# Log-sum-exp over rows: the first load's two transfers cut at one row instead of half a row, the second of them in packets of three rows

## The chip, the cores and the metric

The kernel runs on one core of one Trainium2 chip. The metric is the device time of one execution in microseconds (us), the median of several runs. One core has the engines PE (TensorE), DVE (VectorE), ACT (ScalarE), POOL (GpSimd) and SP (SyncE, which here issues all the transfers), and 16 DMA engines that carry the transfers.

## The reference: what is computed

For each of the 32 x 512 = 16,384 rows of 1,024 float32 numbers, the logarithm of the sum of the exponentials:

```python
max_x = np.max(x, axis=-1, keepdims=True)
return (max_x.squeeze(-1) + np.log(np.sum(np.exp(x - max_x), axis=-1))).astype(np.float32)
```

The input is 67.1 MB, the output 64 KB.

## The kernel before

The maximum isn't taken: the kernel sums the exponentials directly, looks at the end whether a sum or a number is out of bounds, and has a second, slow way (line 328 on) for that case, which doesn't run on these inputs.

The 16,384 rows are laid over 128 partitions, 128 rows each; what the program calls a row of a partition is one of these 1,024 numbers (`d`), 4 KB. The first 112 rows of each partition lie one behind the other in HBM (`x_rows`, line 80), and likewise the last 16 (`x_rest`), so a piece of several rows of one partition is one contiguous stretch in HBM and one in SBUF.

`LOADS` (line 25) is the order of the work, written out by hand: 18 loads, each with its size in rows and what is done with them. The first four have 16 rows (8 MB each), and then they shrink to under half a row. A load goes into a ring of 48 rows a partition (`ring`). ACT takes the exponential of the landed rows in place (line 235), and one of three ways adds them up: R, DVE sums whole rows (line 246); F, POOL first adds the halves of each row (line 240) and DVE sums what is left (line 177); T, DVE adds halves and sums row by row (line 256). The last row is summed by ACT (line 209). Logarithms (lines 275, 288, 290) and two stores end the program.

`load` (line 136) issues each load on SP. Where it overwrites ring space, SP first waits for whoever last read that space (line 139), in practice DVE's sums. Each load has a semaphore of its own, `landed[i]`, to which each transfer adds 16; ACT waits until it has 16 times the number of the load's transfers (line 203), so ACT starts on the first load when both of its parts have landed. Only the first load has two parts (line 141), cut at `FIRST` elements of each partition:

```python
        parts = [(0, FIRST), (FIRST, size)] if i == 0 else [(0, size)]
```

With `FIRST = 512` the first part has 128 x 512 elements (256 KB) and the second 128 x 15,872 (7,936 KB). The transfers of the first three loads (`AHEAD = 3`, four transfers) need no wait; `start_early` (line 387) moves them to the head of SP's program, ahead of the barrier at which the engines start together. They stand there in the order first part, second part, second load, third load.

Of the kernel before, what the change touches and what calls it, by code (L numbers as in the profile page):

```python
# [16 lines left out]
B = 16  # L17
LATE = 119
AHEAD = 3
FIRST = 512  # L20

# [31 lines left out]
def kernel(  # L55
# [30 lines left out]
    def source(e0, size):  # L86
        assert e0 >= W * d or e0 + size <= W * d
        return x_rest[:, e0 - W * d : e0 - W * d + size] if e0 >= W * d else x_rows[:, e0 : e0 + size]
# [8 lines left out]
    def sbuf(name, cols, dtype=fp32, rows=P):  # L97
        return nc.alloc_sbuf_tensor(name, [rows, cols], dtype).ap()

    ring = sbuf("ring", RING * d)  # L100
# [35 lines left out]
    def load(i, here, done_before, size):  # L136
        for a, b, who, at in users:
            if a < here + size and b > here:
                sp.wait(who, at)
        users[:] = [u for u in users if not (u[0] < here + size and u[1] > here)]  # L140
        parts = [(0, FIRST), (FIRST, size)] if i == 0 else [(0, size)]
        return [
            nc.sync.dma_start(  # L143
                out=ring[:, here + a : here + b], in_=source(done_before + a, b - a)
            ).then_inc(landed[i], 16)
            for a, b in parts
        ]
# [38 lines left out]
    here = 0  # L186
    early_sum = 0
    done_before = 0
# [3 lines left out]
    for i, (size, ops) in enumerate(loads):  # L192
# [3 lines left out]
        if any(q < here + size and q + t * d > here for _, t, q, _ in folded):  # L196
            reduce_folded()
        dma = load(i, here, done_before, size)
        if i < AHEAD:
            first_loads.extend(x.ins for x in dma)  # L200
# [3 lines left out]
        for k, (how, s) in enumerate(ops):  # L204
            rows = ring[:, p : p + s * d].rearrange("p (c d) -> p c d", d=d)
            if how in "YZ":
# [3 lines left out]
                    out=last_exp[:, here - p : end - p], in_=ring[:, here:end], func=AF.Exp,  # L210
# [4 lines left out]
                here = end  # L215
# [5 lines left out]
            elif how == "A":  # L221
# [3 lines left out]
                    out=v, in_=v, func=AF.Exp, accum_out=sumexp[:, c : c + 1]  # L225
# [5 lines left out]
            else:  # L231
# [4 lines left out]
                here = upto  # L236
            if how == "F":
# [3 lines left out]
                    out=rows[:, :, 0:H], in0=rows[:, :, 0:H], in1=rows[:, :, H:d], op=ALU.add  # L241
                ))
                folded.append((c, s, p, at))
            elif how == "R":
                dve.wait(act, at)
                who = (dve, dve.did(nc.vector.reduce_sum(  # L246
                    out=sumexp[:, c : c + s], in_=rows, axis=AX.X
                )))
                users.append((p, p + s * d, *who))
            elif how == "T":  # L250
# [3 lines left out]
                for r in range(s):  # L254
                    lo = rows[:, r, 0:H]
                    who = (dve, dve.did(nc.vector.scalar_tensor_tensor(  # L256
                        out=lo, in0=lo, scalar=1.0, in1=rows[:, r, H:d],
# [13 lines left out]
            if c == LATE:  # L271
# [4 lines left out]
                    out=res[:, 0:W], in_=sumexp[:, 0:W], func=AF.Ln  # L276
# [14 lines left out]
        out=res[:, LAST:NC], in_=last_sum, func=AF.Ln, bias=sumexp[:, LAST:NC]  # L291
# [8 lines left out]
        out=clamped[:, LATE:NC], in0=sumexp[:, LATE:NC], scalar=LOW,  # L300
# [10 lines left out]
        out=over[:, 0:half], in0=last_piece[:, 0:half], scalar=CEILING,  # L311
# [16 lines left out]
    with nc.If(all_fine < 1):  # L328
# [5 lines left out]
        for c0 in range(0, NC, RING):  # L334
# [6 lines left out]
            for c1, c2 in ((c0, edge), (edge, c0 + s)):  # L341
                if c1 == c2:
                    continue
                nc.scalar.dma_start(
                    out=ring[:, (c1 - c0) * d : (c2 - c0) * d],
                    in_=source(c1 * d, (c2 - c1) * d),
# [4 lines left out]
                out=neg, in_=v, op=ALU.max, axis=AX.X, negate=True  # L351
# [3 lines left out]
                out=v, in0=v, in1=neg[:, :, None].to_broadcast([P, s, d])  # L355
# [5 lines left out]
                out=sumexp[:, c0 : c0 + s], in_=v, axis=AX.X  # L361
# [71 lines left out]
```

## Time and profile before

| | |
|---|---|
| median of 3 runs | 161.47 us (161.45 to 161.5) |
| the profiled execution | 161.67 us |
| its span in the trace | 160.3 us |
| DVE busy, ACT busy | 114.2 us, 114.5 us |
| POOL busy, PE busy | 37.3 us, 2.2 us |
| share of 16 DMA engines' span in the loads' and stores' queue | 97.7% |
| packets in that queue | 3024, with 67.18 MB |
| ACT starts on the load of 7 rows (4,096 elements and so on) | 130.87 us |
| engines let go by the barrier (DVE's first instruction, ACT's table load) | 2.9 us |

Times within the trace count from the start of the span. A row of a timeline has the start, the length, the engine, the line, the operation with its tiles, how many instructions were merged into the row, and in brackets how long the engine had stood still and for whom. `SPq` is SP's own sequence of instructions: its rows give the time in which SP issued a transfer, not the transfer. DMA packets are counted in the window in which they start, with their whole time, so a short window can show more than 100% of the engines or more GB/s than they move.

### The profile page before, as it was taken

What the parts mean: (1) busy time and instruction counts of PE and PEld (TensorE: products, weight loads), DVE (VectorE), ACT (ScalarE), POOL (GpSimd) and SP (SyncE); (2) the same over time, 40 slices, a digit from 0 to 9 for tenths busy, and PEclk for the clock granted to TensorE, in tenths of its full rate; (3) what the DMA queues carried; (4) which work ended last, traced back from release to release, by engine and by line L of the source; (5) the groups of instructions that cost most, each with busy time, mean ns of one, the idle gap of its engine ahead of it and who ended that gap; (6) DMA issues with size and microseconds to landing.
All of it is one profiled execution on the core that took longest, in us unless ns stands there. A gap on an engine that the chain in (4) does not pass through costs nothing.

```text
span 160.3 us, 221 instructions
## 1 busy us (share of the span) xinstructions
PE 2.2 (1%) x26; PEld 1.1 (1%) x26; DVE 114.2 (71%) x59; ACT 114.5 (71%) x31; POOL 37.3 (23%) x11
## 2 busy tenths in 40 slices
PE   0000000000000000000000000000000000000022
PEld 0000000000000000000000000000000000000011
DVE  0000000009999499994999859959999999999996
ACT  2000059990799708995099949991999989799996
POOL 0000000000000000000000994690004969891000
DMA  8996996996996996996999999999998999999992
GB/s 319 507 491 269 507 523 262 523 523 262 523 507 278 523 507 278 523 507 278 482 441 441 441 425 409 409 409 489 432 432 371 451 416 435 416 413 425 415 410 87
DMA packets 3025, 67.18 MB, mean 419 GB/s; under 512 B 592, under 2 KB 720, under 8 KB 1488
## 3 DMA queue, kind: packets, MB, share of 16 engines
q1 hardware_dynamic: 3024, 67.18, 97.7%
q14 instruction: 1, 0.01, 0.0%
HBM read 67.11 MB, written 0.07 MB: 419 GB/s over the span
## 4 chain that ended last, share of the span: by engine, by line
DMA 52%; ACT 28%; DVE 19%; issue 1%; SPq 1%; PE 0%
DMA ring<-in_x_dram 52%; ACT ring L235 27%; DVE sumexp L246 15%; DVE sumexp L177 2%; DVE ring L256 1%; SPq L143 1%; DVE over L310 0%; PE count L315 0%; ACT res L275 0%; DVE clamped L299 0%; DVE fine L317 0%; DVE sumexp L219 0%
## 5 line engine op out<-in xcount | busy, mean ns | idle before, releaser
L235 ACT ACTIVATE ring<-ring 128x16384 f32<-128x16384 f32 (+16 forms) x23 | 111.7, 4908 | 41.5 <-DMA ring<-in_x_dram 41.5
L246 DVE TENSOR_REDUCE sumexp<-ring 128x16 f32<-128x16384 f32 (+4 forms) x9 | 85.6, 9513 | 41.2 <-ACT ring L235 41.2
L240 POOL TENSOR_TENSOR ring<-ring 128x3072 f32<-128x3072 f32 (+3 forms) x7 | 37.1, 5314 | 107.3 <-ACT ring L235 107.3
L177 DVE TENSOR_REDUCE sumexp<-ring 128x6 f32<-128x3072 f32 (+3 forms) x7 | 18.4, 2657 | 0.0
L256 DVE SCALAR_TENSOR_TENSOR ring<-ring 128x512 f32<-128x512 f32 x15 | 9.6, 687 | 0.4 <-ACT ring L235 0.4
L127 ACT ACT_TABLE_LOAD x1 | 1.3, 1283 | 2.9 <-PEq L64 2.9
L162 PE MATMUL count<-far,bad 128*1 128x1 f32 x2 | 0.2, 164 | 153.1 <-DVE clamped L157 153.1
L128 DVE MEMSET ones<- 128x1 f32 x1 | 0.1, 59 | 2.9 <-PEq L64 2.9
L166 PE MATMUL count<-sumexp,ones 128*1 128x1 f32 x18 | 1.6, 164 | 3.6 <-DVE ring L256 3.6
L256 DVE DVE_READ_ACCUMULATOR ring<-ring 128x1 f32 x15 | 1.2, 81 | 0.0
L209 ACT ACTIVATE last_exp<-ring 128x544 f32<-128x544 f32 (+1 forms) x2 | 1.2, 584 | 0.0
L162 PEld LDWEIGHTS count<-far,bad 128*1 128x1 f32 x2 | 0.1, 80 | 153.1 <-DVE clamped L157 153.1
L166 PEld LDWEIGHTS count<-sumexp,ones 128*1 128x1 f32 x18 | 0.8, 80 | 4.4 <-DVE ring L256 4.4
L310 DVE SCALAR_TENSOR_TENSOR over<-ring 128x240 f32<-128x240 f32 x1 | 0.4, 404 | 0.0
L317 DVE TENSOR_SCALAR fine<-count 1x1 int32<-1x1 f32 x1 | 0.1, 145 | 0.3 <-PE count L315 0.3
L157 DVE SCALAR_TENSOR_TENSOR clamped<-clamped,sumexp 128x119 f32<-128x119 f32 x1 | 0.3, 281 | 0.0
L275 ACT ACTIVATE res<-sumexp 128x112 f32<-128x112 f32 x1 | 0.3, 279 | 0.0
L290 ACT ACTIVATE res<-last_sum,sumexp 128x1 f32<-128x1 f32 x1 | 0.3, 262 | 0.0
L209 ACT ACTIVATION_READ_ACCUMULATOR last_exp<-ring 128x1 f32 x2 | 0.2, 124 | 0.0
L152 DVE TENSOR_SCALAR clamped<-sumexp 128x119 f32<-128x119 f32 x1 | 0.2, 221 | 0.0
L288 ACT ACTIVATE res<-sumexp 128x15 f32<-128x15 f32 x1 | 0.2, 207 | 0.0
L299 DVE SCALAR_TENSOR_TENSOR clamped<-sumexp 128x9 f32<-128x9 f32 x1 | 0.2, 169 | 0.0
(17 smaller groups left out, 1.8 us busy)
## 6 DMA issues: line engine op xcount, KB each, us to landing
ring<-in_x_dram SPq DMA_DIRECT2D x1, 7936.0 KB, 21.5
ring<-in_x_dram SPq DMA_DIRECT2D x1, 6912.0 KB, 23.9
ring<-in_x_dram SPq DMA_DIRECT2D x1, 6400.0 KB, 19.7
ring<-in_x_dram SPq DMA_DIRECT2D x1, 4608.0 KB, 15.9
ring<-in_x_dram SPq DMA_DIRECT2D x1, 3584.0 KB, 24.0
ring<-in_x_dram SPq DMA_DIRECT2D x1, 3072.0 KB, 19.1
ring<-in_x_dram SPq DMA_DIRECT2D x1, 2288.0 KB, 24.1
ring<-in_x_dram SPq DMA_DIRECT2D x1, 1664.0 KB, 20.9
```

Source lines behind the costliest of these rows:

```text
L127: nc.scalar.preload_act_table_set("natural_log_exp_and_others")
L143: nc.sync.dma_start(out=ring[:, here + a : here + b], in_=source(done_before + a, b - a)).then_inc(landed[i], 16)
L157: dve.did(nc.vector.scalar_tensor_tensor(out=clamped[:, 0:LATE], in0=clamped[:, 0:LATE], scalar=0.0, in1=sumexp[:, 0:LATE], op0=ALU.bypass ...
L162: pe.did(nc.tensor.matmul(count, lhsT=bad[:, 0:1], rhs=far, start=True, stop=False))
L166: return pe.did(nc.tensor.matmul(count, lhsT=ones, rhs=sumexp[:, c : c + 1], **kw))
L177: at = dve.did(nc.vector.reduce_sum(out=sumexp[:, c0 : c0 + s0], in_=halves, axis=AX.X))
L209: at = act.did(nc.scalar.activation(out=last_exp[:, here - p : end - p], in_=ring[:, here:end], func=AF.Exp, accum_out=first_sum if how == ...
L235: at = act.did(nc.scalar.activation(out=v, in_=v, func=AF.Exp))
L240: at = pool.did(nc.gpsimd.tensor_tensor(out=rows[:, :, 0:H], in0=rows[:, :, 0:H], in1=rows[:, :, H:d], op=ALU.add))
L246: who = (dve, dve.did(nc.vector.reduce_sum(out=sumexp[:, c : c + s], in_=rows, axis=AX.X)))
L256: who = (dve, dve.did(nc.vector.scalar_tensor_tensor(out=lo, in0=lo, scalar=1.0, in1=rows[:, r, H:d], op0=ALU.mult, op1=ALU.add, accum_out ...
L310: dve.did(nc.vector.scalar_tensor_tensor(out=over[:, 0:half], in0=last_piece[:, 0:half], scalar=CEILING, in1=last_piece[:, half : 2 * half ...
```

## The change

The first part has one row of each partition (4 KB) instead of half a row, and the second 15 rows instead of 15.5. The second part is given a limit of 12,288 bytes for the last dimension of its transfer. The other loads, the waits and the computation are as they were; the new constant and the new argument shift the later lines by one or two.

```diff
-FIRST = 512
+FIRST = 1024
+STEP = 12288
...
         parts = [(0, FIRST), (FIRST, size)] if i == 0 else [(0, size)]
         return [
             nc.sync.dma_start(
-                out=ring[:, here + a : here + b], in_=source(done_before + a, b - a)
+                out=ring[:, here + a : here + b], in_=source(done_before + a, b - a),
+                **({"max_dma_last_dim": STEP} if a else {}),
             ).then_inc(landed[i], 16)
             for a, b in parts
         ]
```

On SP the head of the program is, before (partitions x elements; `ring` is the ring, `in_x_dram` the input; the branch ends the part ahead of the barrier, and the load behind it is the fourth):

```order
L143 DMA ring<-in_x_dram 128x512
L143 DMA ring<-in_x_dram 128x15872
L143 DMA ring<-in_x_dram 128x16384 x2
L428 UNCONDITIONAL_BRANCH
L143 DMA ring<-in_x_dram 128x16384
```

and now:

```order
L144 DMA ring<-in_x_dram 128x1024
L144 DMA ring<-in_x_dram 128x5x3072
L144 DMA ring<-in_x_dram 128x16384 x2
L430 UNCONDITIONAL_BRANCH
L144 DMA ring<-in_x_dram 128x16384
```

The second instruction has five pieces of 3,072 elements (12,288 bytes) for each partition where it had one of 15,872 elements (63,488 bytes). No instruction changed its place, on SP or on another engine.

## Prediction

> **What bounds the kernel now.** I read the page's head and its chain of waits first, then the sums of waits, then ACT's and SP's rows in order of time, and last the DMA packets in short windows.
>
> ```profile
> span 160.3 us, 221 instructions
> DMA 52%; ACT 28%; DVE 19%; issue 1%; SPq 1%; PE 0%
> ACT ring L235 <- DMA ring<-in_x_dram: 41.5, 8, 17.8
> ```
>
> Half of the chain that ends last is transfers into the ring, and ACT, the first engine to touch the data, stood still 41.5 us in 8 waits, all for landings. The longest wait, 17.8 us, is for the load that the change edits. ACT's rows (start, length) show the beat of these landings:
>
> ```profile
> 21.92 13.86 ACT L235 ACTIVATE ring<-ring 128x16384 f32<-128x16384 f32 x1 [17.77 <-DMA ring<-in_x_dram]
> 41.27 13.86 ACT L235 ACTIVATE ring<-ring 128x16384 f32<-128x16384 f32 x1 [5.50 <-DMA ring<-in_x_dram]
> 60.62 13.86 ACT L235 ACTIVATE ring<-ring 128x16384 f32<-128x16384 f32 x1 [5.50 <-DMA ring<-in_x_dram]
> 79.97 13.95 ACT L235 ACTIVATE ring<-ring 128x9216 f32<-128x9216 f32 x2 [5.49 <-DMA ring<-in_x_dram]
> ```
>
> The second, third and fourth loads of 16 rows each come 19.35 us behind the one ahead. The first comes at 21.92, so the start of the program costs 21.92 - 19.35 = 2.57 us over the beat. The change can touch only that excess and the beat of its own load. Next question: does a shift at 21.92 reach the end whole? The chain in order of time (start, length), beginning and end:
>
> ```profile
> 0.00 0.39 SPq L143
> 0.39 0.05 issue
> 0.44 0.42 SPq L143
> 0.86 0.04 issue
> 0.90 40.35 DMA ring<-in_x_dram
> ...
> 72.41 23.88 DMA ring<-in_x_dram
> 96.28 0.02 issue
> ...
> 119.06 19.09 DMA ring<-in_x_dram
> 138.16 0.02 issue
> 138.18 12.34 ACT ring L235 x5
> 150.52 0.18 ACT res L275
> 150.70 6.04 ACT ring L235 x4
> ```
>
> The last landing that ACT waits for ends at 138.16. From there ACT computes without a pause and the tail follows. For a shift to go missing, the transfers would have to stand idle somewhere for want of an issue. SP's issues of the fourth load, of the sixth (12.5 rows), and of the pair whose first lands at 138.16:
>
> ```profile
> 53.06 0.33 SPq L143 DMA_DIRECT2D ring<-in_x_dram  x1
> ...
> 91.76 0.33 SPq L143 DMA_DIRECT2D ring<-in_x_dram  x1
> ...
> 119.06 0.80 SPq L143 DMA_DIRECT2D ring<-in_x_dram  x2
> ```
>
> The fourth load is issued at 53.06, 7.6 us before the third has landed (60.62). The sixth is issued at 91.76, 4.5 us before the fifth lands (the chain's 96.28), and the pair at 119.06 comes 11.8 us before ACT starts on the load of seven rows ahead of it (130.87, the table above). So the transfers always have work queued, and SP's waits (for DVE, which waits for ACT, which waits for landings) move along with the landings. A delay of the first load in all DMA engines therefore goes to the end one for one, and so does a gain.
>
> **The change part by part.** (1) *Bytes*: the same 8.39 MB; no cost. (2) *Packets.* A load row of a partition is now one packet: in the window 24 to 40 us 96 packets carry 6.29 MB, 65,536 bytes each (the first row below). After the change the second part has 128 x 5 = 640 packets where 128 were, over 16 engines 40 in place of 8 each: 32 more per engine, of 12,288 bytes. The first part keeps 8 per engine, twice as long. No transfer of the trace has five packets a partition, but one packet's price by size can be had. The rows behind it are of three more windows (62 to 78, 150.2 to 151.6 and 154.0 to 154.7 us): packets started, megabytes, and the packets' time as a share of 16 engines.
>
> ```profile
> DMA packets 96, 6.29 MB, mean 393 GB/s; under 512 B 0, under 2 KB 0, under 8 KB 0
> ...
> q1 hardware_dynamic: 111, 7.27, 104.9%
> ...
> q1 hardware_dynamic: 80, 0.59, 100.6%
> ...
> q1 hardware_dynamic: 76, 0.29, 101.7%
> ```
>
> The 65,536-byte packet takes 1.049 x 16 us x 16 / 111 = 2419 ns, the one of 7,424 bytes (the load of 1,856 elements) 1.006 x 1.4 x 16 / 80 = 281.7 ns. The slope is (2419 - 281.7) / 58,112 = 0.03678 ns a byte, and 281.7 - 273.1 = 8.6 ns a packet are left. In the last window, of 3,968-byte packets, the records sum to 101.7% of the engines' time: they overlap by 1.7% of some 156 ns, 2.6 ns. So a packet boundary costs between 8.6 - 2.6 = 6.0 and 8.6 ns. I take 6.0, since the overlap is time in which the engine really did both. 32 x 6.0 = **+0.19 us** (bounds +0.19 and +0.28). Nothing hides it: ACT waits for the slowest engine's last packet of this load.
>
> The Trainium skill (DMA: Bandwidth & Descriptors, Why small descriptors are slow) speaks against splitting too: it gives a fixed 3 cycles a packet beside 8 cycles for 256 bytes. By the slope above 8 cycles would be 9.4 ns and 3 cycles 3.5 ns, an estimate from that page that makes 32 x 3.5 = 0.11 us and the sum 161.58. The trace has a boundary at 6.0 to 8.6 ns, and the measurement decides; by either the forecast stays in one class.
>
> (3) *SP's issue.* The four issues ahead of the start-up (two parts, two loads of 16 rows) take 0.39 to 0.43 us each whether they carry 256 KB or 8 MB, but all have 128 packets. One of 640 packets lies between 0.42 us, if the cost is that of the instruction, and 5 x 0.42 = 2.1 us, if it is that of the packets. I take the low end: between 256 KB and 8 MB it did not move, and the nearest rows are all there. SP's two loads behind it are then issued at 0.90 and 1.38 as now; even 1.7 us later they would be in time for a queue busy until 21 us. SP also joins the barrier that lets ACT, DVE and PE start at 2.9 us; ACT needs only its table load (1.3 us) done by 21.92, so 17 us cover that. If the issue grew by all of 1.7 us, the cover of the second part itself would be gone: the first rival.
>
> The Trainium skill (same page, Why a DMA increments its semaphore by 16 and not by 1, the table of cycles per instruction) gives 512 cycles per instruction for a plain copy on the generations before the newest. At the 1.2 GHz that its entry page (Trainium Kernel Development and Optimization, NeuronCore Architecture) gives SyncE that is an estimated 0.43 us, and the rows of 0.39 to 0.43 us agree; by that rule the issue would not grow.
>
> (4) *The longer first part.* What the engines do at the start (window, length, then at the end DMA share and GB/s), and the packets started from 1.0 to 1.8 us:
>
> ```profile
> core 0: us, PE busy (x) PEld busy (x) DVE busy (x) ACT busy (x) POOL busy (x), PEclk, DMA share, GB/s
> 1.00:4.50 3.50, 0.00 (x0) 0.00 (x0) 0.15 (x4) 1.28 (x1) 0.00 (x0) 1.00 0.99 365
> 4.50:6.84 2.34, 0.00 (x0) 0.00 (x0) 0.00 (x0) 0.00 (x0) 0.00 (x0) 1.00 1.00 434
> ...
> q1 hardware_dynamic: 54, 0.11, 66.5%
> ```
>
> Nothing moves before 1.0 us; from 1.0 to 4.5 packets of 365 GB/s start while the engines read as busy, and from 4.5 on the full 434. The loss is 3.5 x (434 - 365) / 434 = 0.56 us for the mean engine. Part of it is in the short packets: 54 of them took 0.665 x 0.8 x 16 / 54 = 158 ns each, where 2,048 x 0.0368 + 8.6 = 84 are due; 74 x 54 / 16 = 0.25 us an engine. The other 0.31 us is in the first long packet of each engine. Is this a price of the first bytes (latency, which any packets pay) or of these packet sizes? The trace of before cannot say. Bounds: -0.56 us if all of it goes, +0.56 if each part of it doubles with a doubled first part. I take 0: after 4.5 us packets of 63,488 bytes and of 65,536 run at full rate, and so do those of 7,424, so the size alone brings no loss; what is particular about these packets is that they come first.
>
> Sum: the profiled execution was 161.67 us, 1.37 around its span of 160.3; 161.67 + 0.19 = 161.86. It stands 0.20 above the median of the runs, 161.47, which the forecast is for: **161.66 us**, 0.1% slower, less than a measurement of this kernel can tell from no change if that is put at 0.2% (0.32 us).
>
> **Rivals.** *First: the second part's packets come late* (slower). If SP's issue takes 2.1 us, it ends at 0.44 + 2.1 = 2.54. The first packet of all came 1.0 - 0.39 = 0.61 us behind its issue's end, so these would come at 3.15. The engines leave the first part earlier, as three short windows of before show:
>
> ```profile
> 1.75:2.00 0.25, 0.00 (x0) 0.00 (x0) 0.00 (x0) 0.00 (x0) 0.00 (x0) 1.00 2.28 885
> 2.25:2.50 0.25, 0.00 (x0) 0.00 (x0) 0.00 (x0) 0.00 (x0) 0.00 (x0) 1.00 5.74 2327
> 2.50:4.00 1.50, 0.00 (x0) 0.00 (x0) 0.15 (x4) 1.13 (x1) 0.00 (x0) 1.00 0.00 0
> ```
>
> More GB/s than the engines can move means that long packets start: from 1.75 us on at the earliest, and by 2.5 all have. 8 x 2,048 bytes more at 0.0368 ns each add 0.60: 2.35 to 3.1. They would stand still 0.05 to 0.8 us; with 0.5 the time is 161.47 + 0.19 + 0.5 = 162.16. It decides from an issue of 3.15 - 0.61 - 0.44 - 0.8 = 1.3 us on. For it: no row has an issue of this kind, and SP was seen to be held up by a long queue, three issues near 136 us taking 2.51 us where four near 126 took 1.77:
>
> ```profile
> 126.59 1.77 SPq L143 DMA_DIRECT2D ring<-in_x_dram  x4
> 136.01 2.51 SPq L143 DMA_DIRECT2D ring<-in_x_dram  x3
> ```
>
> Against: the issue did not change from 256 KB to 8 MB.
>
> *Second: the start-up loss goes* (faster). If the short packets are slow because each pays for itself, 8 longer ones move twice the bytes for the same price, and if 16 long packets that start together block one another, packets of a fifth part their length let the engines get out of step early. All of the mean engine's loss gone gives 161.47 + 0.19 - 0.56 = 161.10. The slowest engine, which sets the landing, has more to lose: 21.92 - 1.0 - 19.35 = 1.57 us lie between full rate and ACT's start, the landing's notice in it. For it: the rows 365 and 434. Against: the same bytes at the same addresses are read first.
>
> *Third: the packets aren't cut.* The five pieces of a partition lie side by side in both memories and could go as one packet: 161.45. Against it, the program's instruction carries 5 x 3072.
>
> **How the numbers follow.** Forecast 0.45, its own range 161.35 to 161.95 (the packet price's ends and 0.25 us of a shuffled start); first rival 0.22, second 0.27, third 0.06. The range must reach into both rivals: 161.0 to 162.25. Faster by over 0.2% (under 161.15): most of the second, 0.22. Slower (over 161.79): the first, and a tail of the forecast, 0.27. Within: 0.51.
>
> **What would show it.** Right: the page counts 512 packets more (3025 to 3537); ACT's first row starts at about 22.1, the next 19.35 behind it; the second issue on SP stays near 0.42; the window from 1.0 to 4.5 us again starts clearly less than 434 GB/s. Wrong by the first rival: an issue of over 1.3 us and a stretch without packets between 2.3 and 3.2. Wrong by the second, which decides from 400 GB/s on: ACT's first row before 21.7 with more than that from 1.0 to 4.5. Wrong in the argument itself: a first landing that moves while the end does not.

## The result and the profile after

| | before | after |
|---|---|---|
| median of 17 runs each | 161.63 us | 161.91 us |
| ratio, 95% interval | | 1.0021 [1.0014, 1.0028] |
| the profiled execution, its span | 161.67, 160.3 us | 161.82, 160.5 us |

The change costs 0.28 us by the medians and 0.34 us by the ratio, whose interval is 0.23 to 0.45 us. The forecast was +0.19 us with a range from 161.0 to 162.25. The time lies in the range. The ratio lies just past 0.2%, on the side to which the prediction gave a chance of 0.27; it gave 0.51 to a change within 0.2%.

The page of the changed kernel, its packets and its queue:

```profile
span 160.5 us, 221 instructions
DMA packets 3537, 67.18 MB, mean 419 GB/s; under 512 B 592, under 2 KB 720, under 8 KB 1488
q1 hardware_dynamic: 3536, 67.18, 97.9%
```

The queue has 3536 packets where it had 3024: the 512 more that the cut should make. So the pieces are not put together again, and the third rival is out. ACT's rows in order of time:

```profile
22.07 13.86 ACT L237 ACTIVATE ring<-ring 128x16384 f32<-128x16384 f32 x1 [17.77 <-DMA ring<-in_x_dram]
41.43 13.86 ACT L237 ACTIVATE ring<-ring 128x16384 f32<-128x16384 f32 x1 [5.50 <-DMA ring<-in_x_dram]
60.78 13.86 ACT L237 ACTIVATE ring<-ring 128x16384 f32<-128x16384 f32 x1 [5.50 <-DMA ring<-in_x_dram]
```

The first load comes 0.15 us later than in the profile of before, and the beat of the others is the old one (19.36 and 19.35). The end of the chain of waits, as of before (start, length):

```profile
119.24 19.08 DMA ring<-in_x_dram
138.32 0.02 issue
138.34 12.32 ACT ring L237 x5
150.66 0.19 ACT res L277
150.85 6.04 ACT ring L237 x4
```

Everything is 0.14 to 0.18 us later than its row of before: the shift at the first landing reaches the end, neither lost nor grown. That the two profiled executions differ by 0.15 and the medians by 0.28 is within what single executions of one kernel scatter (161.45 to 161.81 before); the profiled execution after, 161.82, is also near the fastest of its 17 (161.79 to 162.19).

ACT waits for the slowest of the 16 DMA engines. The trace also keeps the time at which each engine's share of the first load landed: 21.25 to 21.90 us in before, 21.47 in the mean, and 21.60 to 22.05 after, 21.84 in the mean. So the mean engine is 0.37 us later and the slowest 0.15, since the engines land closer together.

SP's issue of the cut transfer, and the start-up window (length, then at the end DMA share and GB/s):

```profile
0.43 0.44 SPq L144 DMA_DIRECT2D ring<-in_x_dram  x1
```

```profile
1.00:4.50 3.50, 0.00 (x0) 0.00 (x0) 0.15 (x4) 1.28 (x1) 0.00 (x0) 1.00 1.00 350
```

The issue of 640 packets takes 0.44 us where that of 128 took 0.42, so the first rival is out as well. ACT's first row is not before 21.7 but later than it was, and the start-up window is not faster (350 against 365 GB/s), so the second rival, which needed both, did not come about.

### The profile page after: what moved, and what is told of

The parts are those of the page before. It is cut to its first block, busy times and chain, and to the rows that moved or that the text cites. A ratio compares the mean times of both kernels' runs of the same rounds, so it can differ in the third digit from the quotient of the medians.

```text
span 160.5 us, 221 instructions
## 1 busy us (share of the span) xinstructions
PE 2.2 (1%) x26; PEld 1.1 (1%) x26; DVE 114.2 (71%) x59; ACT 114.5 (71%) x31; POOL 37.3 (23%) x11
## 3 DMA queue, kind: packets, MB, share of 16 engines
q1 hardware_dynamic: 3536, 67.18, 97.9%
## 4 chain that ended last, share of the span: by engine, by line
DMA 52%; ACT 28%; DVE 19%; issue 1%; SPq 1%; PE 0%
DMA ring<-in_x_dram 52%; ACT ring L237 27%; DVE sumexp L248 15%; DVE sumexp L179 2%; DVE ring L258 1%; SPq L144 1%; DVE over L312 0%; PE count L317 0%; ACT res L277 0%; DVE clamped L301 0%; DVE fine L319 0%; DVE sumexp L221 0%
```

## The experiments

The theory at the outset: each packet boundary (one packet more for the same bytes) costs its DMA engine some nanoseconds wherever it stands, and the start-up loss doesn't depend on the packets. The rivals put the 0.28 us on the longer first part, on a start that the cut makes better or worse, or on SP. Each run was timed in turn with the kernel before on the same chip; the medians of before were 161.53 us (the first four) and 161.59 us (the other four).

### The longer first part alone

```diff
-FIRST = 512
+FIRST = 1024
```

> Only the longer first part: one row of each partition (4 KB packets), the second part of 15 rows as one packet of 61,440 bytes each. Theory (each packet boundary costs 6.0 ns of its DMA engine, and the start-up loss stays): no packet more than before, so 161.63 plus or minus 0.1, ACT's first row at 21.9 to 22.0, the next 19.35 behind. Rival one (the time of the change comes from the longer first part, whose 4 KB packets were slow at the start): 161.9, as the whole change. Rival two (the cut is what helps the start and the longer part costs): over 161.9.

Measured: 161.55 us, ratio 1.0004 [0.9995, 1.0013]. That is 0.08 us less to 0.21 us more than before, so the longer part is not the whole effect, and no cost of its own is seen. Its rows of ACT:

```profile
21.75 13.86 ACT L235 ACTIVATE ring<-ring 128x16384 f32<-128x16384 f32 x1 [17.59 <-DMA ring<-in_x_dram]
41.10 13.86 ACT L235 ACTIVATE ring<-ring 128x16384 f32<-128x16384 f32 x1 [5.49 <-DMA ring<-in_x_dram]
```

The first landing is 0.32 us ahead of the changed kernel's 22.07, and the only difference between the two is the cut. Each of these numbers is one profiled execution; before's is 21.92.

### The cut alone

```diff
-                out=ring[:, here + a : here + b], in_=source(done_before + a, b - a)
+                out=ring[:, here + a : here + b], in_=source(done_before + a, b - a),
+                **({"max_dma_last_dim": 15872} if a else {}),
```

> The first part as before (512 elements), the second part of 15.5 rows cut into 4 packets of 15,872 bytes a partition: 24 packets more for each DMA engine. Theory: 24 x 6.0 ns = +0.14 us, 161.77. Rival one (the longer first part is the cause): 161.63, as before. Rival two (the cut removes the stalls of the first long packets): 161.63 + 0.14 less up to 0.3, so 161.5.

Measured: 161.8 us, ratio 1.0018 [1.0009, 1.0027]: +0.27 us, about the whole effect, with the first part as before and 24 boundaries where the change has 32. For 24 that is 11 ns each, and the interval (0.15 to 0.44 us) allows 6 to 18. The first rival said no change and the second 161.5; both are out.

### The second part in packets of one row

The edit is that of the change with `"max_dma_last_dim": 4096`: 15 packets for each partition.

> First part of one row as in the change, the second in 15 packets of 4,096 bytes a partition: 112 packets more for each DMA engine than before. Theory: 112 x 6.0 ns = +0.67 us over before, 162.30, and ACT's first row 0.67 later than before's 21.92, so 22.6. Rival one (the longer first part alone costs): 161.9, as the change. Rival three (what costs is SP's issue of a cut transfer): SP's second issue grows well over 0.44 us and a stretch without packets shows; the time is then not linear in the number of packets.

Measured: 162.57 us, ratio 1.0062 [1.0049, 1.0076]: +1.0 us for 112 boundaries, 9.3 ns each (7.1 to 11), where the theory had said 0.67. The sign and the growth with the count are right; the price is too low. The issue of the cut transfer stays at 0.44 us (first row below), so the third rival is out. SP's next issue and ACT's first rows show something else:

```profile
0.43 0.44 SPq L143 DMA_DIRECT2D ring<-in_x_dram  x1
0.91 8.15 SPq L143 DMA_DIRECT2D ring<-in_x_dram  x1
```

```profile
11.40 1.28 ACT L127 ACT_TABLE_LOAD   x1 [11.40 <-PEq L64]
22.83 13.86 ACT L236 ACTIVATE ring<-ring 128x16384 f32<-128x16384 f32 x1 [10.14 <-DMA ring<-in_x_dram]
```

The uncut transfer behind the cut one takes 8.15 us to issue, SP comes to the barrier that much later, and ACT's table load starts at 11.40 instead of 2.87. ACT still waits 10.14 us for the landing, so the late start is not what the load waits for here.

### The second load in packets of one row

```diff
+                **({"max_dma_last_dim": 4096} if i == 1 else {}),
```

> The first load as before; the second load of 16 rows, which starts to move at about 21 us, in 16 packets of 4,096 bytes a partition instead of one of 65,536: 120 packets more for each DMA engine, far from the start. Theory: 120 x 6.0 ns = +0.72 us, 162.35; ACT's first row stays at 21.9, the second comes 20.07 behind it instead of 19.35. Rival one or any cause that lies in the start-up: 161.63, as before.

Measured: 165.41 us, ratio 1.0241 [1.0227, 1.0255], +3.88 us. A cause in the start-up alone would have given no change and the theory 0.72 us; neither gives this time. SP's and ACT's rows:

```profile
1.39 26.97 SPq L143 DMA_DIRECT2D ring<-in_x_dram  x1
...
61.85 0.33 SPq L143 DMA_DIRECT2D ring<-in_x_dram  x1
```

```profile
29.42 1.28 ACT L127 ACT_TABLE_LOAD   x1 [29.42 <-PEq L64]
30.71 27.60 ACT L236 ACTIVATE ring<-ring 128x16384 f32<-128x16384 f32 x2
61.64 13.86 ACT L236 ACTIVATE ring<-ring 128x16384 f32<-128x16384 f32 x1 [3.33 <-DMA ring<-in_x_dram]
83.65 13.95 ACT L236 ACTIVATE ring<-ring 128x9216 f32<-128x9216 f32 x2 [8.15 <-DMA ring<-in_x_dram]
```

The issue behind the cut transfer now takes 26.97 us. It is still ahead of the barrier, so ACT and DVE don't start before 29.4 us; ACT begins at 30.71 on data that had landed by 21.8, DVE sums later, and ring space comes free later. SP issues the fourth load at 61.85 instead of 53.06, when the third has landed (61.6) and no transfer is left in the queue, and it is late (83.65 instead of 79.97). So a stretch without queued work, which the prediction found nowhere in before, does come about when the barrier is late enough. This is a reading of the rows; the next run tests it.

### The same cut, but issued behind the barrier

The edit of the run before, and

```diff
-AHEAD = 3
+AHEAD = 1
```

> The second load in 16 packets of 4,096 bytes a partition, as in the run that came out at +3.88 us, but only the first load is issued ahead of the barrier (AHEAD = 1), so an SP that is held up by its queue holds up no barrier. Theory (each packet boundary costs its DMA engine 8.5 to 9.3 ns, as the third load's landing in that run and the first load's in the 15-packet run say, and the rest of the +3.88 was the barrier): ACT's table load is back near 3 us, ACT starts on the first load at about 21.9, and the time is 161.55 + 120 x 8.5 to 9.3 ns = +1.02 to 1.12, 162.6. Rival (short packets themselves cost 32 ns each when they are in the queue behind a load): again about 165.4.

Measured: 162.91 us, ratio 1.0077 [1.0063, 1.0091]: +1.32 us instead of +3.88. SP is held about as long as before (26.17 us, first block), but behind the barrier, and ACT starts on time; so most of the rest was the barrier. The kernel with AHEAD = 1 and no cut was not run, so what that edit does by itself is not shown. SP's issue and ACT's rows:

```profile
2.36 26.17 SPq L143 DMA_DIRECT2D ring<-in_x_dram  x1
```

```profile
1.93 1.28 ACT L127 ACT_TABLE_LOAD   x1 [1.93 <-PEq L64]
22.05 13.86 ACT L236 ACTIVATE ring<-ring 128x16384 f32<-128x16384 f32 x1 [18.83 <-DMA ring<-in_x_dram]
42.50 13.86 ACT L236 ACTIVATE ring<-ring 128x16384 f32<-128x16384 f32 x1 [6.59 <-DMA ring<-in_x_dram]
61.87 13.86 ACT L236 ACTIVATE ring<-ring 128x16384 f32<-128x16384 f32 x1 [5.51 <-DMA ring<-in_x_dram]
```

The cut load comes 20.45 us behind the one ahead of it, the next 19.37 again. 20.45 - 19.35 = 1.10 us over 120 boundaries are 9.2 ns each. The first landing is 0.13 later than in before's profile; together that is 1.23 of the 1.32 us.

### The fourth load in packets of half a row

```diff
+                **({"max_dma_last_dim": 2048} if i == 3 else {}),
```

> The fourth load, which is issued at 53 us, long after the start, in 32 packets of 2,048 bytes a partition: 248 packets more for each DMA engine. Theory of the boundary at 8.5 to 9.3 ns: +2.1 to 2.3 us, 163.75, ACT's rows up to 60.62 unmoved and the fourth (79.97) later by that. With the 6.0 ns of the prediction: +1.49, 163.05. Rival (SP, held at the next issue until the queue has room, makes later loads late): ACT's rows after the fourth load slip further.

Measured: 164.06 us, ratio 1.0147 [1.0132, 1.0163]: +2.47 us, a little over the 2.1 to 2.3 of the revised price and far over the 1.49 of the prediction's. ACT's rows of the second, third and fourth loads:

```profile
41.28 13.86 ACT L236 ACTIVATE ring<-ring 128x16384 f32<-128x16384 f32 x1 [5.50 <-DMA ring<-in_x_dram]
60.79 13.86 ACT L236 ACTIVATE ring<-ring 128x16384 f32<-128x16384 f32 x1 [5.65 <-DMA ring<-in_x_dram]
82.43 13.95 ACT L236 ACTIVATE ring<-ring 128x9216 f32<-128x9216 f32 x2 [7.78 <-DMA ring<-in_x_dram]
98.78 11.82 ACT L236 ACTIVATE ring<-ring 128x6144 f32<-128x6144 f32 x2 [2.40 <-DMA ring<-in_x_dram]
```

The fourth comes 21.64 us behind the third: (21.64 - 19.35) / 248 = 9.2 ns a boundary, the same as for packets twice as long. The load behind it is on the old beat (16.35 us; 16.34 in before). SP's next issue took 0.77 us instead of 0.33 and made nothing late, so the rival is out:

```profile
72.42 0.77 SPq L143 DMA_DIRECT2D ring<-in_x_dram  x1
```

The expectation that the third load would not move was wrong: it comes 19.51 us behind the second, 0.16 late, though its packets are whole. SP issues the cut transfer at 53.07, and the packets that were then on their way took longer; in the window 51.9 to 52.8 us:

```profile
DMA packets 15, 0.98 MB, mean 1092 GB/s; under 512 B 0, under 2 KB 0, under 8 KB 0
...
q1 hardware_dynamic: 15, 0.98, 266.5%
```

2.665 x 0.9 us x 16 / 15 = 2558 ns each; in before the packets under the issue at 53.06 (window 52.2 to 53.0) took 3.034 x 0.8 x 16 / 16 = 2427:

```profile
DMA packets 16, 1.05 MB, mean 1311 GB/s; under 512 B 0, under 2 KB 0, under 8 KB 0
...
q1 hardware_dynamic: 16, 1.05, 303.4%
```

The packets ahead of these in the same trace took 2418 to 2425 ns. So the packets beside the issue of 4,096 others were some 0.13 us slower; that the issue is the cause is read from the coincidence in one execution. It would also fit the 0.13 us of the run before, where 2,048 packets are issued at 1.93 us beside the first load. The third load's 0.16 and the fourth's 2.29 are 2.45 of the 2.47 us.

### The first load in one transfer, and a first part of four rows

```diff
-        parts = [(0, FIRST), (FIRST, size)] if i == 0 else [(0, size)]
+        parts = [(0, size)]
```

> The first load as one transfer of 16 rows, 65,536 bytes a packet, with nothing in front. Theory (the start-up loss belongs to the first bytes and not to the packet size): 161.55 plus or minus 0.15, less 8 boundaries x 9 ns = 0.07. Rival (the short packets of the first part are what is slow): the mean engine gains 0.25 us, 161.3. Rival (the short first part pays, since long packets that start together block one another): 161.8 or more.

Measured: 161.7 us, ratio 1.0005 [0.9996, 1.0014], 0.06 us less to 0.23 more than before. No gain of 0.25 us shows, so the first rival is out; a small part of the second is not excluded.

```diff
-FIRST = 512
+FIRST = 4096
```

> First part of four rows (16 KB packets), second of 12 rows uncut (48 KB packets); no more packets than before. Theory (size doesn't matter at the start): 161.55 plus or minus 0.15. Rival (short packets slow): 161.3. Rival (a longer first part loses): 161.8.

Measured: 161.6 us, ratio 1.0001 [0.9992, 1.001], 0.13 us less to 0.16 more; both rivals are out. The first rows of ACT, of the one transfer and of the four rows:

```profile
21.94 13.86 ACT L235 ACTIVATE ring<-ring 128x16384 f32<-128x16384 f32 x1 [18.26 <-DMA ring<-in_x_dram]
```

```profile
21.80 13.86 ACT L235 ACTIVATE ring<-ring 128x16384 f32<-128x16384 f32 x1 [17.55 <-DMA ring<-in_x_dram]
```

With packets of 64, 16, 4 and 2 KB at the start, the first landing is at 21.94, 21.80, 21.75 and 21.92. The loss only changes its place. The 16 packets that open the one transfer (window 1.0 to 2.4 us) and the 128 of the four rows (1.0 to 6.3 us):

```profile
q1 hardware_dynamic: 16, 1.05, 224.1%
```

```profile
q1 hardware_dynamic: 128, 2.10, 104.9%
```

In the one transfer each engine's first packet takes 2.241 x 1.4 x 16 / 16 = 3.14 us against a steady 2.42, 0.72 us more. In the other the 16 KB packets take 1.049 x 5.3 x 16 / 128 = 695 ns against 611 due (16,384 x 0.03677 + 9), 8 x 84 ns = 0.67 us an engine. For before the same count takes the 8 short packets and the first long one of each engine (window 1.0 to 2.5 us):

```profile
q1 hardware_dynamic: 160, 1.28, 230.0%
```

They take 2.300 x 1.5 = 3.45 us an engine, where 8 x 84 + 2343 ns = 3.02 us are due: 0.43 us, less than the 0.56 that the prediction took from the GB/s of its window.

None of the eight versions is faster than before by more than its interval, so no run beat both kernels.

## Why the prediction was right, and where its size was off

**The bound and the way to the end**: right. The first landing moved and everything behind it moved by as much (0.15 us at 22.07, 0.16 at 138.34). No row of ACT or SP absorbed it.

**The packets' term**: the mechanism was right and its price too low. The prediction worked out 8.6 ns for a boundary from packet times and then took off 2.6 for overlapping records, leaving 6.0: "I take 6.0, since the overlap is time in which the engine really did both." That step failed. Landings, which need no record of a packet, give 9.2 ns twice in mid-stream (120 and 248 boundaries), and 32 x 9.2 = 0.29 us agrees with what was measured (0.28, interval 0.23 to 0.45, with the prediction's 0.19 outside). The stated upper end, 0.28, was the better number. The first load says the same if all 16 engines are taken: their landings have a mean of 21.47 to 21.60 us in the seven runs whose first load is uncut (21.52 over the seven), and of 21.77, 21.84 and 22.63 us with 24, 32 and 112 boundaries more, some 10 ns each. The overlap was read from a window of 0.7 us, in which packets are counted with their whole time if they start inside: its edges alone move the share by more than the 1.7% on which the step rested, and two windows of before close by read 102.3% (154.6 to 155.4 us) and 97.4% (155.5 to 156.1).

Of the 0.25 us between the forecast of 161.66 and the measured 161.91, 0.16 is that before's median was 161.47 in the three runs that the forecast started from and 161.63 in the 17 beside the change; only 0.09 is the price.

The Trainium skill's 3 cycles a packet (DMA: Bandwidth & Descriptors, Why small descriptors are slow), an estimated 3.5 ns, would have made 0.11 us of the change. The runs have 9.2 ns, and the measurement decides: the page's figure is not the whole price of a boundary here.

**SP's issue**: right. 0.44 us for 640 packets, 0.44 for 1,920 (the 15-packet run): it goes by the instruction, and the first rival's 1.3 us did not come. But the prediction's cover for SP ("17 us") was the right thing to look at for the wrong transfer: what gets long is the issue behind a transfer of many packets. With 40 packets an engine it did not happen; with 120 it took 8 us, and with 128 behind a whole load 27.

**The start-up loss**: the choice of 0 was right as far as the runs can tell, and the reason given for it ("what is particular about these packets is that they come first") held in three runs of other sizes. By the packet records the start loses 0.43 to 0.63 us an engine in the four runs that have before's first load, and 0.57 in the changed kernel. The size of the loss, 0.56 us for before, was read too high. The view was weaker than the argument: GB/s of a window counts packets by their start, so 365, 350 and the 431 GB/s of the longer first part alone say more about where long packets begin than about the loss:

```profile
1.00:4.50 3.50, 0.00 (x0) 0.00 (x0) 0.15 (x4) 1.28 (x1) 0.00 (x0) 1.00 1.16 431
```

That run passes the half of the prediction's test that asks for over 400 GB/s, with a first landing (21.75) just short of the other half (before 21.7), and its time is that of before.

What stays open is why the first 0.4 to 0.7 us of transfer is lost in any form. The runs show only that neither the packets' size nor the split moves the time by more than some 0.2 us. Open too is what the narrower landings are worth: with a cut first load the 16 engines land within 0.34 to 0.45 us of one another (three runs), uncut within 0.50 to 0.75 (seven).

## What to carry to other kernels

Where transfers set the pace, count packets on the slowest DMA engine: each boundary cost 9.2 ns here, whether the packets had 2 or 4 KB, and cutting one load out of 18 in five cost 0.2% with nothing to set against it. Price such a term from landings of whole loads, 19.35 us apart, rather than from packet records in short windows. And before a transfer of many packets is issued ahead of a barrier, look at the issue behind it: SP can stand there for many us (8 and 27 here), and all engines that wait at the barrier with it.

## What the runs showed of the hardware that was not expected

- SP's issue is held while many packets are pending: 8.15 us behind 120 packets an engine, and 26.97 us behind 128 that themselves stood behind a load. The issue of the many packets is itself not held (0.38 to 0.44 us). By the packet records four held issues (8.15, 1.24, 26.97 and 26.17 us) ended when some 90 packets an engine were unfinished, the issue's own 8 among them. It isn't one fixed count: the 0.77 us issue ended with 106 left, behind packets of 2 KB, and one of 1.56 us at 136.96 in before with 71.
- Beside the issue of 4,096 packets the packets in flight took 2558 ns, and 2427 beside that of 128 (one execution each).
- The first packets of the program lose 0.43 to 0.72 us an engine, in 2 KB, 4 KB, 16 KB and 64 KB packets alike.
